# Entry of the feed-forward part of a decoder step: first token forms ahead of the first pair, the third tile on single banks, negated weight copies ahead of their casts

## The chip, the cores and the metric

The kernel runs on one core of one Trainium2 chip. The metric is the time of one execution in device microseconds (us), lower is better; three executions of the kernel before gave a median of 1043.3 us. A core has TensorE (PE, matrix products into PSUM banks), VectorE (DVE), ScalarE (ACT), GpSimd (POOL) and SyncE (SP); the last two issue transfers here, SP plain loads and POOL accumulating ones.

## The reference

One layer of a hybrid decoder trunk, for 512 prompt tokens and 8 sample tokens (520 columns in all), width 1024. After a mixing part of four branches and a cross attention it ends with

```
h3 = rms_norm(x, norm_ffn_g)
x = x + jnp.square(jax.nn.relu(h3 @ w_up)) @ w_down        # w_up 1024 x 4096, w_down 4096 x 1024
```

The change is at the beginning of this last line. Everything ahead of it, and the caches that the layer returns, is computed as before.

## The kernel before, in words

**Numbers in two parts.** Every matrix product is computed from a high and a low part of each factor (float32r): `wh` is the weight cast, `wl` the weight less `wh`, and likewise `hi` and `lo` for tokens. `mm3` (L260) does high by high, high by low, low by high, each for two halves of 260 columns: six products for one slice of 128 rows. A weight tile of 128 x 1024 has eight slices: 48 products.

**How weights come.** `weights` (L165) keeps LA = 3 tiles ahead in a fixed order: ..., `wxo` 0 to 3, `wup` 0 to 3, `wdn` 0, 2, 1, 3, then pairs. `split_weights` (L211) loads a tile `w` from SP and makes `wh` on ACT (L219). For most tiles DVE then subtracts (`low`, L178). For `wdn` ACT writes the negated weight, rounded to float32r, into `wl` behind the cast (L221, `scale=-1.0`), and a transfer issued by POOL adds the exact weight to it (L222, `accum_op=add`), so that the difference remains. Three buffers each for `w`, `wh` and `wl`: a tile's parts can be written when the tile three places earlier has been used.

**The entry of the feed-forward part** (L1527 to L1540). After the eight output tiles of `wxo`, whose residuals (L1190 to L1199) also give the token tiles `x2s`, `rstd` computes the norm's factor `Rf`. `pair` multiplies `wup` 0 and 1 slice by slice in turn into two tiles of the pool `pg` (two tiles of two PSUM banks each). `run` does `wup` 2 and then `wup` 3, each into a tile of `pg`. Each tile has a post-step, `post_up`: relu on ACT (L1423), times `Rf` on DVE (L1424), square on ACT (L1417), high and low part (L145, L146). A post-step is traced only when the next tile's products have been traced (`take`, `advance`). Then `down(0, c)` multiplies the four resulting token slices with `wdn` c; each weight tile has two halves n = 0 and 1, into a tile of `pg` and into two single banks of the pool `pm` (three banks in all).

**Token forms.** From the second group on, `up_pair` computes two `wup` tiles at once from sums and differences of token quarters. `forms` (L1392) prepares them in four steps, each with two multiplications (L1396), four additions (L1404 to L1407) and four splits into high and low parts. The steps are traced with `next(made)`: the first between the pair and the third tile, the second between the third and the fourth, the others behind.

**What sets the order.** A planner orders the instructions of each engine ahead of the run, by simulating them with costs of its own: of those that are ready it takes the one with the highest priority, which is the place in the trace. Inside `tc.high_priority(offset=60)` the place counts as 60 earlier; nested, the offsets add up. `advance` traces a post-step in such a block, and `pin` ties DVE instructions that were traced behind the first DVE instruction of a post-step to stay behind it, except those in `free` (the weight subtractions). On the chip each engine then runs its list strictly in order. In the planned list of the kernel before, `wdn` 0 has only its first two slices (24 products) ahead of the first slices of `wdn` 2; its third and fourth follow.

Of the kernel before, what the change touches and what calls it, by code (L numbers as in the profile page):

```python
# [12 lines left out]
AF = mybir.ActivationFunctionType  # L13
ALU = mybir.AluOpType
# [12 lines left out]
AHEAD = 60  # L27
# [70 lines left out]
def layer(ctx: ExitStack, tc: tile.TileContext, I: dict, O: dict):  # L98
    nc = tc.nc
    V, S, PE, SP, GP = nc.vector, nc.scalar, nc.tensor, nc.sync, nc.gpsimd  # L100
# [11 lines left out]
    def gtile():  # L112
        return pg.tile([P, 2, 512], F32, tag="g", name="g")

    def mtile():
        return pm.tile([P, 512], F32, tag="m", name="m")

    def dtile():
        return pd.tile([P, 512], F32, tag="d", name="d")
# [4 lines left out]
    def HL(dt=F32R, shape=None):  # L124
        return hp.tile(shape or [P, NT], dt, tag="hl", name="hl", bufs=HLB)
# [8 lines left out]
    def two(t):  # L134
        return t[:, 0:NT].rearrange("p (a b) -> p a b", a=2)

    def gv(ps):
        return ps[:, :, 0:H2]
# [38 lines left out]
    def low(wl, w, wh):  # L177
        free.add(V.tensor_tensor(out=wl, in0=w, in1=f(wh), op=ALU.subtract).ins.name)  # L178
# [32 lines left out]
    def split_weights(name, i):  # L211
        if name == "pair":
            return split_pair(i)
        src = I[name][i]
        w = wp.tile([P, KT, P], F32, tag="w", name="w", bufs=WB[0])
        SP.dma_start(out=w, in_=src.rearrange("p (k c) -> p k c", k=KT))
        wh = wp.tile([P, KT, P], F32R, tag="wh", name="wh", bufs=WB[1])
        wl = wp.tile([P, KT, P], F32R, tag="wl", name="wl", bufs=WB[2])
        S.copy(wh, w)  # L219
        if name == "wdn":  # L220
            S.activation(wl, w, AF.Copy, scale=-1.0)  # L221
            GP.dma_start(out=wl, in_=src.rearrange("p (k c) -> p k c", k=KT), accum_op=ALU.add)  # L222
        else:
            low(wl, w, wh)
        return wh, wl

# [32 lines left out]
    def mm3(outs, wh, wl, xh, xl, first, last):  # L259

        for n, (w, x) in enumerate(((wh, xh), (wh, xl), (wl, xh))):
            for o, sl in outs:
                m = PE.matmul(o, lhsT=w, rhs=x[sl], start=first and n == 0, stop=last and n == 2)  # L263
        return m
# [4 lines left out]
    def banks(ps):  # L269
        return [p[:, 0:H2] for p in ps] if isinstance(ps, list) else [ps[:, i, 0:H2] for i in range(2)]  # L270

    def gemm(ps, W, xs, first=True, last=True, k0=0, apart=False):

        wh, wl = W
        outs = [(p, sl) for p, sl in zip(banks(ps), (A0, A1))]
        for o in [outs[:1], outs[1:]] if apart else [outs]:
            for i, (xh, xl) in enumerate(xs):
                PE_last[0] = mm3(o, wh[:, k0 + i], wl[:, k0 + i], xh, xl, first and i == 0, last and i == len(xs) - 1)
# [59 lines left out]
    ps = dtile()  # L338
# [4 lines left out]
    halves = (slice(0, H2), slice(H2, NT))  # L343
# [33 lines left out]
    def Rtile():  # L377
        return tp.tile([P, NT], F32, tag="R", name="R", bufs=1)
# [40 lines left out]
    def advance():  # L419

        fresh[0] = False
        new = pending[-1]
        pin()
        n = len(nc.cur_bb.bb.instructions)
        with tc.high_priority(offset=AHEAD):
            alive = next(new, True) is None
            evac[0] = next((i for i in nc.cur_bb.bb.instructions[n:] if i.engine == mybir.EngineType.DVE), evac[0])
        pending[:] = onward(pending[:-1]) + [new] * alive
        flows[:] = onward(flows)
# [14 lines left out]
    def take(post):  # L444

        if fresh[0]:
            advance()
        pending.append(post)
        fresh[0] = True

    def run(name, i, src, post, steps=0, k0=0, W=None, apart=False):

        ps = [mtile(), mtile()] if apart else gtile()
        W = W or weights(name, i)
        gemm(ps, W, src, k0=k0, apart=apart)
        take(post(ps))
        step(steps)
        return W

    def pair(names, src, posts):  # L460

        ps = [gtile() for n in names]
        Ws = [weights(*n) for n in names]
        for k in range(KT):
            for p, (wh, wl) in zip(ps, Ws):
                gemm(p, (wh[:, k:], wl[:, k:]), src[k:k + 1], first=k == 0, last=k == KT - 1)
        for p, post in zip(ps, posts):
            take(post(p))
# [162 lines left out]
    def step(n=1):  # L631
        for _ in range(n):
            next(dec, None)
# [589 lines left out]
    pss = dtile()  # L1223
# [138 lines left out]
    x2, x2s = [None] * KT, [None] * KT  # L1362
# [15 lines left out]
    Rf = Rtile()  # L1378
    ups = [[None] * 4 for g in range(8)]
# [11 lines left out]
    def forms():  # L1391

        for k in range(4):
            n, m, t, u = T(), T(), T(), T()
            for o, i in ((n, k), (m, k + 4)):
                V.scalar_tensor_tensor(out=o, in0=x2[i], scalar=col("gffn", i), in1=Rf, op0=ALU.mult, op1=ALU.mult)  # L1396
            B11, B12, B21, B22 = n[:, A0[1]], n[:, A1[1]], m[:, A0[1]], m[:, A1[1]]
            if k % 2 == 0:
                b11 = form(2)
            sl = slice(k % 2 * H2, k % 2 * H2 + H2)  # L1400
            hilo(B11, b11[0][:, sl], b11[1][:, sl])
            X["B11", k] = b11[0][:, sl], b11[1][:, sl]
            N1, T2, T3, T4 = t[:, A0[1]], t[:, A1[1]], u[:, A0[1]], u[:, A1[1]]
            V.tensor_tensor(out=N1, in0=B11, in1=B12, op=ALU.subtract)  # L1404
            V.tensor_tensor(out=T2, in0=B22, in1=N1, op=ALU.add)
            V.tensor_tensor(out=T3, in0=B22, in1=B12, op=ALU.subtract)
            V.tensor_tensor(out=T4, in0=T2, in1=B21, op=ALU.subtract)  # L1407
            for src, names in ((t, ("N1", "T2")), (u, ("T3", "T4")), (m, ("B21", "B22"))):
                hi, lo = form(2)
                hilo(src, hi, lo)  # L1410
                for j, s in zip(names, (A0[1], A1[1])):
                    X[j, k] = hi[:, s], lo[:, s]
            yield

    def rest(r, hl):

        S.activation(r, r, AF.Square)  # L1417
        hilo(r, *hl)

    def post_up(i):  # L1420
        def post(ps):
            r = T()
            S.activation(two(r), gv(ps), AF.Relu)  # L1423
            V.tensor_tensor(out=r, in0=r, in1=Rf, op=ALU.mult)  # L1424
            ups[0][i] = HL(), HL()
            rest(r, ups[0][i])
            yield
        return post

# [54 lines left out]
    def post_down(g, c):  # L1484
        def post(ps):
            t = x2[c]
            if isinstance(ps, list):
                for p, sl in zip(banks(ps), halves):
                    V.tensor_tensor(out=t[:, sl], in0=p, in1=t[:, sl], op=ALU.add)
                    if g == 7 and c == KT - 1:  # L1490
                        SP.dma_start(out=O["yT"][c][:, sl], in_=t[:, sl])
            else:
                V.tensor_tensor(out=two(t), in0=gv(ps), in1=two(t), op=ALU.add)
            if g == 7 and c < KT - 1:
                SP.dma_start(out=O["yT"][c], in_=t)
            yield
        return post

    def down(g, cp):

        W = weights("wdn", 4 * g + cp)
        cs = (2 * cp, 2 * cp + 1)
        pss = [gtile(), [mtile(), mtile()]]

        def part(n, ks, first, last):
            for i, k in enumerate(ks):
                gemm(pss[n], (W[0][:, 4 * n:], W[1][:, 4 * n:]), ups[g][k:k + 1], first=first and i == 0,
                     last=last and i == len(ks) - 1, k0=k)

        if cp == CP[0]:  # L1510
            late = 2 if g else 3
            for n in range(2):
                part(n, [k for k in range(4) if k != late], True, False)
            for n in range(2):
                part(n, (late,), False, True)
                take(post_down(g, cs[n])(pss[n]))
        elif g == 7 and cp == CP[-1]:
            part(0, range(4), True, True)
            take(post_down(g, cs[0])(pss[0]))
            gemm(pss[1], (W[0][:, 4:], W[1][:, 4:]), ups[g], apart=True)  # L1520
            take(post_down(g, cs[1])(pss[1]))
        else:
            for n in range(2):
                part(n, range(4), True, True)
                take(post_down(g, cs[n])(pss[n]))
# [2 lines left out]
        rstd(ones, [acc], D, T(), Rf)  # L1528
    first_pair = split_pair(2)
    made = forms()  # L1530
    pair([("wup", 0), ("wup", 1)], x2s, [post_up(0), post_up(1)])
    next(made)
    run("wup", 2, x2s, post_up(2))
    next(made)
    run("wup", 3, x2s, post_up(3))
    go()
# [109 lines left out]
```

## Time and profile before

| | us |
|---|---|
| median of three runs | 1043.3 (1042.77 to 1044.19) |
| profiled execution, whole | 1040.07 |
| its span, first to last instruction | 1038.4 |
| PE busy in it | 1020.9 (98%) |
| DVE busy | 669.4 (64%) |
| ACT busy | 525.8 (51%) |
| POOL busy | 170.3 (16%) |

The page's times come from one profiled execution; the run's own time lies 1.67 us above the span. In the views by order of time each line begins with the start and the duration in us, and a bracket at its end says how long the engine had been idle and what released it. The feed-forward part takes the stretch from about 683 us to the end; its entry, with the four `wup` tiles, that from 683 to about 707.

### The profile page before, as it was taken

What the parts mean: (1) busy time and instruction counts of PE and PEld (TensorE: products, weight loads), DVE (VectorE), ACT (ScalarE), POOL (GpSimd) and SP (SyncE); (2) the same over time, 40 slices, a digit from 0 to 9 for tenths busy, and PEclk for the clock granted to TensorE, in tenths of its full rate; (3) what the DMA queues carried; (4) which work ended last, traced back from release to release, by engine and by line L of the source; (5) the groups of instructions that cost most, each with busy time, mean ns of one, the idle gap of its engine ahead of it and who ended that gap; (6) DMA issues with size and microseconds to landing.
All of it is one profiled execution on the core that took longest, in us unless ns stands there. A gap on an engine that the chain in (4) does not pass through costs nothing.

```text
span 1038.4 us, 21502 instructions
## 1 busy us (share of the span) xinstructions
PE 1020.9 (98%) x8266; PEld 941.1 (91%) x8266; DVE 669.4 (64%) x1231; ACT 525.8 (51%) x858; POOL 170.3 (16%) x299
## 2 busy tenths in 40 slices
PE   8999999999999999999999999999999999999998
PEld 7978787888988898889999986899999999999998
DVE  6766766776556665534676678689756566566643
ACT  7756567854222225412545577567636355363541
POOL 1333442231223332230100000000001000010000
PEclk9999999999999999999999999999999999999999
DMA  8877986574457776772523548146457564565544
GB/s 264 339 235 253 260 284 199 194 224 153 154 192 244 243 231 218 221 248 88 195 82 103 187 163 286 74 132 151 125 143 162 142 163 123 145 162 142 122 103 123
DMA packets 62089, 188.87 MB, mean 182 GB/s; under 512 B 10145, under 2 KB 12962, under 8 KB 61858
## 3 DMA queue, kind: packets, MB, share of 16 engines
q0 software_dynamic: 25408, 84.97, 30.7%
q1 hardware_dynamic: 36578, 102.52, 29.0%
q8 instruction: 65, 1.06, 0.4%
q14 instruction: 38, 0.31, 0.1%
HBM read 181.85 MB, written 5.61 MB: 181 GB/s over the span
## 4 chain that ended last, share of the span: by engine, by line
PE 89%; ACT 4%; DVE 4%; DMA 1%; issue 1%; SPq 0%; DVEq 0%; ACTq 0%
PE g L263 60%; PE m L263 15%; PE d L600 3%; PE d L548 2%; PE d L263 2%; PE m L286 2%; PE g L1171 1%; ACT wh L219 1%; DVE wl L178 1%; DMA wl<-in_wdn 1%; DMA hl<-in_xT 1%; PE m L653 1%; PE m L701 0%; PE m L687 0%; PE m L708 0%
## 5 line engine op out<-in xcount | busy, mean ns | idle before, releaser
L263 PE MATMUL g<-hl,wh 128*128 128x260 f32 x3664 | 606.6, 285 | 3.9 <-DVE sd L570 1.5
L263 PEld LDWEIGHTS g<-hl,wh 128*128 128x128 f32 x3664 | 510.3, 188 | 22.2 <-issue 7.0
L263 PE MATMUL g<-hl,wl 128*128 128x260 f32 x1832 | 384.6, 283 | 1.7 <-DMA wl<-in_wdn 1.7
L263 PEld LDWEIGHTS g<-hl,wl 128*128 128x128 f32 x1832 | 288.4, 188 | 2.2 <-DMA wl<-in_wdn 1.9
L219 ACT CAST wh<-w 128x1024 fp32r<-128x1024 f32 x126 | 132.0, 1048 | 283.6 <-PE g L263 115.8
L178 DVE TENSOR_TENSOR wl<-w,wh 128x1024 fp32r<-128x1024 f32 (+1 forms) x122 | 141.3, 1160 | 37.1 <-ACT wh L219 33.9
L263 PE MATMUL m<-hl,wh 128*128 128x260 f32 x792 | 134.8, 282 | 0.0
L263 PEld LDWEIGHTS m<-hl,wh 128*128 128x128 f32 x792 | 114.0, 188 | 0.0
L222 POOL DMA_DIRECT2D wl<-in_wdn x32 | 27.7, 866 | 491.2 <-DVE t L1396 196.0
L513 POOL DMA_DIRECT2D pg<-in_vc x128 | 69.0, 539 | 176.1 <-issue 79.4
L513 POOL DMA_DIRECT2D pg<-in_kc x128 | 69.3, 541 | 145.7 <-issue 100.1
L263 PE MATMUL m<-hl,wl 128*128 128x260 f32 x396 | 92.4, 282 | 0.0
L475 DVE TENSOR_TENSOR t<-g,R 128x520 f32<-128x520 f32 x48 | 33.4, 695 | 64.1 <-PE g L263 64.1
L263 PEld LDWEIGHTS m<-hl,wl 128*128 128x128 f32 x396 | 66.2, 188 | 0.0
L146 DVE TENSOR_TENSOR hl<-t,hl 128x520 fp32r<-128x520 f32 (+3 forms) x67 | 43.6, 654 | 20.6 <-ACT hl L145 20.2
L197 ACT CAST wh<-p 128x1024 fp32r<-128x1024 f32 x28 | 29.4, 1049 | 40.4 <-PE m L263 28.1
L145 ACT CAST hl<-t 128x520 fp32r<-128x520 f32 (+3 forms) x67 | 39.0, 589 | 18.3 <-DVE t L486 11.3
L197 ACT CAST wh<-w 128x1024 fp32r<-128x1024 f32 (+1 forms) x28 | 23.3, 835 | 39.8 <-PE m L263 30.1
L882 DVE SCALAR_TENSOR_TENSOR hl<-uc,cols,hl 128x512 f32<-128x512 f32 x60 | 41.2, 746 | 0.0
L178 DVE TENSOR_TENSOR wl<-p,wh 128x1024 fp32r<-128x1024 f32 x28 | 34.3, 1224 | 7.9 <-ACT wh L197 7.9
L191 DVE TENSOR_TENSOR p<-w 128x512 f32<-128x512 f32 x28 | 19.0, 688 | 26.6 <-DMA w<-in_wup 26.6
L221 ACT ACTIVATE wl<-w 128x1024 fp32r<-128x1024 f32 x32 | 33.7, 1054 | 0.0
(301 smaller groups left out, 1156.7 us busy)
## 6 DMA issues: line engine op xcount, KB each, us to landing
pg<-in_kc POOLq DMA_DIRECT2D x128, 256.0 KB, 4.5
pg<-in_vc POOLq DMA_DIRECT2D x128, 256.0 KB, 3.9
w<-in_win SPq DMA_DIRECT2D x56, 512.0 KB, 4.5
w<-in_wup SPq DMA_DIRECT2D x32, 512.0 KB, 3.5
w<-in_wdn SPq DMA_DIRECT2D x32, 512.0 KB, 3.6
wl<-in_wdn POOLq DMA_DIRECT2D x32, 512.0 KB, 7.8
w<-in_wo SPq DMA_DIRECT2D x8, 512.0 KB, 3.2
hl<-in_cmk SPq DMA_DIRECT2D x16, 256.0 KB, 5.2
```

Of the source, the lines that this page charges most:

```text
L145: S.copy(hi, src)
L146: V.tensor_tensor(out=lo, in0=src, in1=f(hi), op=ALU.subtract)
L178: free.add(V.tensor_tensor(out=wl, in0=w, in1=f(wh), op=ALU.subtract).ins.name)
L197: S.copy(h, src)
L219: S.copy(wh, w)
L221: S.activation(wl, w, AF.Copy, scale=-1.0)
L222: GP.dma_start(out=wl, in_=src.rearrange("p (k c) -> p k c", k=KT), accum_op=ALU.add)
L263: m = PE.matmul(o, lhsT=w, rhs=x[sl], start=first and n == 0, stop=last and n == 2)
L475: V.tensor_tensor(out=two(t), in0=gv(ps), in1=two(Rt), op=ALU.mult)
L513: last.append(GP.dma_start(out=dst, in_=src[bass.ds(pid, 1)].rearrange("o p f -> p o f")))
L600: PE.matmul(ps[32 * i:32 * i + 32, :], lhsT=Dt[:, n, :], rhs=vp[:, i, :], start=n == 0, stop=n == 15)
L882: V.scalar_tensor_tensor(out=y[:, 0:NP], in0=u[:, k:k + NP], scalar=cw[:, k:k + 1], in1=y[:, 0:NP], op0=ALU.mult, op1=ALU.add)
```

## The change

`wup` 1 and 2 get their low part like `wdn` does, from a negated copy and an accumulating transfer; and where that is done, copy and transfer are traced ahead of the cast. The first step of the forms is traced ahead of the pair. The third tile goes to two single banks of `pm` (the parameter `apart`, which also split the order of the products and was not used here, gives way to `single`). `post_up` reads either kind of tile, and its instructions stand in a further high-priority block inside that of `advance`. In the first down tile of a group, the slices of group 0 go in three rounds, (0, 1), (2), (3), each over both halves, where it was (0, 1, 2) and (3); later groups keep (0, 1, 3) and (2).

```
-        S.copy(wh, w)
-        if name == "wdn":
+        added = name == "wdn" or (name == "wup" and i in (1, 2))
+        if added:
             S.activation(wl, w, AF.Copy, scale=-1.0)
             GP.dma_start(out=wl, in_=src.rearrange("p (k c) -> p k c", k=KT), accum_op=ALU.add)
-        else:
+        S.copy(wh, w)
+        if not added:
             low(wl, w, wh)
...
-        ps = [mtile(), mtile()] if apart else gtile()
+        ps = [mtile(), mtile()] if single else gtile()
         W = W or weights(name, i)
-        gemm(ps, W, src, k0=k0, apart=apart)
+        gemm(ps, W, src, k0=k0)
...
             r = T()
-            S.activation(two(r), gv(ps), AF.Relu)
-            V.tensor_tensor(out=r, in0=r, in1=Rf, op=ALU.mult)
-            ups[0][i] = HL(), HL()
-            rest(r, ups[0][i])
+            with tc.high_priority(offset=AHEAD):
+                if isinstance(ps, list):
+                    for p, sl in zip(banks(ps), halves):
+                        S.activation(r[:, sl], p, AF.Relu)
+                else:
+                    S.activation(two(r), gv(ps), AF.Relu)
+                V.tensor_tensor(out=r, in0=r, in1=Rf, op=ALU.mult)
+                ups[0][i] = HL(), HL()
+                rest(r, ups[0][i])
             yield
...
-            late = 2 if g else 3
-            for n in range(2):
-                part(n, [k for k in range(4) if k != late], True, False)
-            for n in range(2):
-                part(n, (late,), False, True)
-                take(post_down(g, cs[n])(pss[n]))
+            parts = ((0, 1, 3), (2,)) if g else ((0, 1), (2,), (3,))
+            for ks in parts:
+                for n in range(2):
+                    part(n, ks, ks is parts[0], ks is parts[-1])
+                    if ks is parts[-1]:
+                        take(post_down(g, cs[n])(pss[n]))
...
     made = forms()
+    next(made)
     pair([("wup", 0), ("wup", 1)], x2s, [post_up(0), post_up(1)])
-    next(made)
-    run("wup", 2, x2s, post_up(2))
+    run("wup", 2, x2s, post_up(2), single=True)
     next(made)
     run("wup", 3, x2s, post_up(3))
```

## Rows read from the trace of the kernel before

**Rows 1.** The page's first part: busy us, share of the span, instructions.

```profile
PE 1020.9 (98%) x8266; PEld 941.1 (91%) x8266; DVE 669.4 (64%) x1231; ACT 525.8 (51%) x858; POOL 170.3 (16%) x299
```

**Rows 2.** Stretches: length, busy us of each engine, granted clock, queues' share, GB/s.

```profile
696.00:714.00 18.00, 16.28 (x134) 16.08 (x135) 17.75 (x35) 16.58 (x28) 2.63 (x3) 1.00 0.72 161
...
750.00:1038.00 288.00, 285.20 (x2376) 284.98 (x2374) 168.85 (x296) 133.20 (x174) 22.50 (x26) 1.00 0.57 138
```

**Rows 3.** Waits of PE, 640 to 1038: for whom, us, times, longest.

```profile
PE g L263 <- DMA wl<-in_wdn: 1.7, 1, 1.7
PE g L263 <- ACT t L1423: 0.7, 1, 0.7
```

**Rows 4.** PE in order of time: the pair's end and the third tile's start.

```profile
693.62 0.64 PE L263 MATMUL g<-hl,wh 128*128 128x260 f32 x4
...
694.35 0.65 PE L263 MATMUL g<-hl,wh 128*128 128x260 f32 x4
...
695.90 0.74 PE L263 MATMUL g<-hl,wh 128*128 128x260 f32 x4 [0.67 <-ACT t L1423]
```

**Rows 5.** PE in order of time: the first products of `wdn` 2.

```profile
710.38 0.64 PE L263 MATMUL g<-hl,wh 128*128 128x260 f32 x4
712.73 0.51 PE L263 MATMUL g<-hl,wl 128*128 128x260 f32 x2 [1.72 <-DMA wl<-in_wdn]
```

**Rows 6.** The chain that ended last, in time: start, us, what (issue to landing).

```profile
705.72 6.97 DMA wl<-in_wdn
```

**Rows 7.** ACT in order of time: `wdn` 2's cast and copy, third relu.

```profile
702.57 1.05 ACT L219 CAST wh<-w 128x1024 fp32r<-128x1024 f32 x1
...
704.36 1.06 ACT L221 ACTIVATE wl<-w 128x1024 fp32r<-128x1024 f32 x1
705.32 0.58 ACT L1423 ACTIVATE t<-g 128x520 f32<-128x520 f32 x1
```

**Rows 8.** DVE in order of time: norm's factor, a weight subtraction, first post-step.

```profile
692.02 0.70 DVE L299 SCALAR_TENSOR_TENSOR R<-t 128x520 f32<-128x520 f32 x1
695.38 1.23 DVE L178 TENSOR_TENSOR wl<-w,wh 128x1024 fp32r<-128x1024 f32 x1 [2.65 <-ACT wh L219]
696.52 0.69 DVE L1424 TENSOR_TENSOR t<-t,R 128x520 f32<-128x520 f32 x1
```

**Rows 9.** DVE in order of time: low parts of the third and fourth tokens.

```profile
709.05 0.69 DVE L146 TENSOR_TENSOR hl<-t,hl 128x520 fp32r<-128x520 f32 x1
...
711.00 0.69 DVE L146 TENSOR_TENSOR hl<-t,hl 128x520 fp32r<-128x520 f32 x1
```

**Rows 10.** ACT in order of time: the cast of `wup` 1 and what follows.

```profile
676.91 1.05 ACT L219 CAST wh<-w 128x1024 fp32r<-128x1024 f32 x1
...
678.82 0.63 ACT L1198 ACTIVATE t<-x 128x520 f32<-128x520 f32 x1
```

**Rows 11.** PE in order of time: the first six products of `wup` 1.

```profile
684.02 0.64 PE L263 MATMUL g<-hl,wh 128*128 128x260 f32 x4
684.50 0.52 PE L263 MATMUL g<-hl,wl 128*128 128x260 f32 x3
```

**Rows 12.** L222, issue to landing: all 32, that at 720.4, that at 1003.5.

```profile
DMA to landing us min/median/max: 5.4/7.8/8.6
...
DMA to landing us min/median/max: 7.9/7.9/7.9
...
DMA to landing us min/median/max: 5.4/5.4/5.4
```

**Rows 13.** SP in order of time: plain weight loads issued.

```profile
680.59 0.33 SPq L216 DMA_DIRECT2D w<-in_wdn  x1
...
705.44 0.33 SPq L184 DMA_DIRECT2D w<-in_wup  x1
...
720.05 0.33 SPq L216 DMA_DIRECT2D w<-in_wdn  x1
...
1000.66 0.33 SPq L216 DMA_DIRECT2D w<-in_wdn  x1
```

More of the change, by code (lines that the diff above doesn't have):

```diff
@@ L449, in take, with run @@
         fresh[0] = True
-    def run(name, i, src, post, steps=0, k0=0, W=None, apart=False):
-        ps = [mtile(), mtile()] if apart else gtile()
+    def run(name, i, src, post, steps=0, k0=0, W=None, single=False):
+        ps = [mtile(), mtile()] if single else gtile()
         W = W or weights(name, i)
-        gemm(ps, W, src, k0=k0, apart=apart)
+        gemm(ps, W, src, k0=k0)
         take(post(ps))
```

## The prediction

> **What bounds the kernel now.** I read the page's first part, then the stretches, the waits of TensorE behind 640 us, and only then the engines in order of time around the entry of the feed-forward part. The first part has TensorE (PE) busy nearly throughout, the other engines at most two thirds [rows 1]. From 750 us to the end its products stand back to back at the granted clock 1.00, its higher level of 2.4 GHz [rows 2]: what is won or lost ahead of that point reaches the end undiminished. So only PE's waits count. Two of them lie at the entry: 0.7 us for the first tile's relu and 1.7 us for the negated weights of a `wdn` tile [rows 3]. Those two are what the change can take away, and as matmul ends are modelled I size both by starts. Six products take 0.72 to 0.73 us (693.62 to 694.35), 0.12 each [rows 4].
>
> - Wait A: the pair's last group starts at 694.35, so the third `wup` tile was due at 695.07 and started at 695.90: **0.83 us**. Both double-bank tiles of `pg` were held by the pair until ScalarE (ACT) had read the first [rows 3, 4].
> - Wait B: the four high products start at 710.38, so the first low one was due at 710.86 and started at 712.73: **1.87 us** [rows 5]. That is the second down weight (`wdn` 2; the order is 0, 2, 1, 3), whose accumulating transfer was issued at 705.72 and landed 6.97 us later, at 712.69 [rows 6].
>
> **The change part by part.**
>
> *Third tile on single banks.* It takes two tiles of `pm` and no longer needs the pair's relu: wait A goes, −0.83. The relu becomes two instructions for one of 0.58 us [rows 7], at most 0.6 us more on ACT, beside 5.8 us of the fourth tile's products. What is late next is that tile's weights, and they are given the same room as before relative to the pair's end. The fourth tile needs the double bank of the first, free with the relu some 5 us before.
>
> *First forms ahead of the pair, the post-step at doubled priority.* No instruction is added. VectorE (DVE) had the norm's factor at 692.72 (692.02 + 0.70) and then stood idle 2.65 us, because the forms were traced behind the first tile's post-step and pinned behind its multiply at 696.52 [rows 8]. Now they can fill that hole. By itself this is worth nothing on PE: the third tile's tokens were complete at 709.74 and the fourth's at 711.69 [rows 9], while PE could have begun the third slice of `wdn` 0 at 710.38 at the earliest and, twelve products on, the last at 711.82. The tokens were in time; it was the issue order that had `wdn` 2 ahead of them. What the part changes is that order. I cost it at nothing; were it to delay the first post-step by a whole form (2.65 us of cover gone), the tokens of the first slices are still due only 11.5 us behind the pair.
>
> *Slices (0,1), (2), (3) and the negated copy ahead of the cast.* The two go together against wait B. ACT did the cast of `wdn` 2 at 702.57, two casts of forms behind it, and the negated copy only at 704.36 [rows 7]: the copy first starts the transfer at least 1.05 us sooner. And with tokens ready for the planner, all 48 products of `wdn` 0 (5.76 us) stand ahead of `wdn` 2, not 24. Third tile from 695.07 to 700.83, fourth to 706.59, `wdn` 0 to 712.35, low product of `wdn` 2 due at 712.83 (all plus the stall below). The transfer landed 11.03 us behind the end of the third tile (712.69 less 701.66); the same distance is 711.86, or 710.8 with the copy first. It is in time by 1 to 2 us: −1.87. If only the third slice comes ahead, it is due at 711.39, still between those two.
>
> *`wup` 1 and 2 by negated copy and accumulating transfer.* This removes two DVE subtractions of 1.23 us [rows 8], which DVE could spare (PE waits for none of them), and adds two ACT copies of 1.06 us [rows 7], two issues on GpSimd (POOL) and 1 MB through the queues. ACT has idle time there, so the copies cost nothing by themselves. The landing does. `wup` 2 finds its buffers one weight later, 5.8 us on at 682.7, and is due 12 us behind that: harmless. `wup` 1 is the second tile of the pair itself. Its buffers come free with the third `wxo` weight; ACT started its cast at 676.91 [rows 10]. Now the copy starts there: ready at 677.97, issued 0.30 us later as at wait B (copy done at 705.42, issue at 705.72) [rows 6, 7], 678.27. Its first low product ran at 684.50 [rows 11]. Issue to landing over all 32 such transfers is 5.4 to 8.6 us [rows 12]: landed between 683.7 and 686.9, a stall of **0 to 2.4 us**. Which end? The change also lets SyncE (SP) send the first `wdn` load at about 679.0 (677.97 and 1.05 for the cast) rather than 680.59, since the load's buffer now waits for a cast and not for a subtraction [rows 13]; so one plain load runs beside it. With one such load beside, issued within 0.4 us, the transfers took 7.0 and 7.9; the one at 1003.5, with the last plain weight load issued at 1000.66, took 5.4 [rows 6, 12, 13]. I take 7.5: landed 685.77, product at 685.81 with the 0.04 us that wait B shows (712.69 to 712.73), stall **1.3 us**.
>
> Would the planner see that and put the first tile's products ahead? In the order of before it set the low product of `wdn` 2 76 products (9.1 us) behind the end of the third tile, with its copy ending 3.76 us behind that end; so my estimate is that it counts at most 5.3 us from copy to landing, where the chip took 7.3. For `wup` 1 that is 683.3, ahead of 684.50: it keeps the order, and PE waits. Everything behind shifts with it, the sums above too, so the margins stay. The granted clock was 1.00 through wait B's stretch too [rows 2]; so a shorter stall is costed at its length alone.
>
> Here the Trainium skill speaks for the change. Its page "DMA: Bandwidth & Descriptors", section "Anatomy of one DMA — SWDGE (gpsimd) path", fits a transfer issued by GpSimd as about 2.0 us plus its bytes over 436 GB/s; for 512 KB that is an estimate of 3.2 us, landed at 681.5, no stall and a sum of −2.7 us. The trace disagrees by these rows (none of 32 accumulating ones under 5.4 us), so the result it gives stands below as a rival only.
>
> **Sum:** −0.83 − 1.87 + 1.3 = **−1.4 us**. Against the profiled execution (1040.07 us, its span 1038.4 and 1.67 around it) that is 1038.7. The median of the runs is 3.2 us above that execution; the same −1.4 on it gives **1041.9**.
>
> **The rivals.**
>
> 1. *No stall.* The transfer takes the 5.4 us of the undisturbed one, or the planner, seeing it late, lets the first tile's remaining 42 products (5.0 us) run ahead. Then −2.7: **1040.6**. For: the shortest time seen is enough (683.7 against 684.50), and the queue was free of other loads but one. Against: that one load.
> 2. *The order of `wdn` 2 stays.* The change doesn't do what it says for wait B, as the tokens are still late in the planner's reckoning, where ACT has two copies more to do. Then at most the whole 1.87 remains: −0.83 + 1.3 = +0.5, **1043.8**. Against: 2.65 us of DVE freed.
> 3. *Slower.* The negated copy of `wup` 1 goes behind the fifth residual's two ACT operations, which end at 679.45 [rows 10], because it now has to find both its buffer and the planner's turn. Then it is ready at 680.51, issued 680.81, and with 8.6 us lands at 689.41: a stall of 4.9 us, −2.7 + 4.9 = +2.2, **1045.5**. It decides from a landing behind 687.2 on, where the stall exceeds both waits. Against: ACT took the cast at once at 676.91, with equal priority.
>
> **How the numbers follow.** Forecast 0.45, rival 1 0.25, rival 2 0.15, rival 3 0.12, other orderings 0.03. The forecast's own range, from a stall of 0.6 to 2.4, is 1041.2 to 1043.0. A measurement of this kernel tells 0.2% from no change, 2.1 us: 1041.2 and 1045.4. Below the first lie four fifths of rival 1 (0.20) and 0.08 of the forecast: faster 0.28. Above the second lie three quarters of rival 3 and the odd ones: slower 0.12. The rest, 0.60, is within. The range leaves out a tenth at each end: from 1040.2, rival 1 with 0.4 us for the stray of a median (the three runs lie 1.4 apart), to 1044.9, between rivals 2 and 3.
>
> **What would show it.** In the waits of PE behind 640 us: no wait for the relu of L1423 (now another line); no wait for `wl<-in_wdn`; a new one for `wl<-in_wup` of about 1.3 us, at 684.5. In POOL's order of time: two issues at about 678.3 and 684. On DVE: the forms of the first token slice starting at about 692.7 plus the stall. In ACT's order: each negated copy ahead of its cast, from `wdn` 0 on. The prediction is wrong if `wl<-in_wup` never stops PE, if it stops it for over 2.4 us, or if a wait stands at the down products that was not there before, such as the single banks being asked for by `wdn` 0 while the third tile's halves are unread.

## The result, and the profile after

The changed kernel is **slower**: 1051.88 us (median of 4 runs, 1051.66 to 1055.17) against 1043.03 us of the kernel before on the same chip (4 runs, 1041.18 to 1044.19), a ratio of 1.0098 with a 95% interval of 1.0082 to 1.0114. The prediction, 1041.9 in a range of 1040.2 to 1044.9, was wrong in sign and by 10 us. The profiled execution took 1051.72 us, its span 1050.0: 11.6 us more than the one of before. The traces lie further apart than the medians (8.9 us) because the profiled execution of before, at a mean granted clock of 1.00, is 3.0 us under that kernel's median, while that of the changed kernel (0.995) is at its own.

The page's first part (beside [rows 1]) hardly shows it. PE is busier by 6.6 us with the same 8266 instructions, and DVE by 3 us less:

```profile
PE 1027.5 (98%) x8266; PEld 945.4 (90%) x8266; DVE 666.3 (63%) x1229; ACT 526.8 (50%) x861; POOL 171.9 (16%) x301
```

The waits of PE behind 640 us tell where to look (waiting line and what ended the wait; us, times, longest). Both rows of [rows 3] are gone. In their place stand one wait for the accumulating transfer of a `wup` tile, and five for a residual addition of VectorE:

```profile
PE m L264 <- DVE hl L1495: 5.2, 5, 1.8
PE g L264 <- DMA wl<-in_wup: 3.6, 1, 3.6
```

**The stall at the pair.** PE in order of time, beside [rows 4, 11]; behind the stall six products take 1.2 to 1.3 us where they took 0.72:

```profile
684.36 0.64 PE L264 MATMUL g<-hl,wh 128*128 128x260 f32 x4
688.58 0.63 PE L264 MATMUL g<-hl,wl 128*128 128x260 f32 x3 [3.58 <-DMA wl<-in_wup]
689.04 0.95 PE L264 MATMUL g<-hl,wh 128*128 128x260 f32 x4
...
690.23 1.07 PE L264 MATMUL g<-hl,wh 128*128 128x260 f32 x4
...
700.82 0.64 PE L264 MATMUL m<-hl,wh 128*128 128x260 f32 x4
```

The stretches around it, with the columns of [rows 2]: granted clock and the queues' share are the two numbers ahead of the last.

```profile
684.00:689.00 5.00, 1.42 (x12) 1.21 (x11) 4.37 (x7) 2.55 (x4) 0.86 (x1) 1.00 0.99 229
689.00:692.00 3.00, 3.00 (x17) 3.00 (x16) 0.00 (x0) 0.00 (x0) 0.00 (x0) 0.53 0.99 317
692.00:695.00 3.00, 3.00 (x21) 2.81 (x21) 0.00 (x0) 2.02 (x4) 0.00 (x0) 0.90 0.28 108
695.00:698.00 3.00, 3.00 (x27) 3.00 (x27) 1.96 (x3) 0.90 (x2) 0.00 (x0) 1.00 0.00 0
```

What is to be seen: the low product was due at 684.84, four high ones behind 684.36, and came at 688.58, **3.74 us** late. Behind it the granted clock is 0.53, its lower level of 1.2 GHz, until into the next stretch. The third tile starts at 700.82 with no wait, where 695.07 was its due time in the kernel before. Of these 5.75 us, 0.34 lie ahead of the pair (684.36 against 684.02 [rows 11]), 3.74 are the stall, and the remaining **1.7** are the clock.

Why the transfer was late stands in three orders of time and the chain. ACT and SP (beside [rows 10, 13]), then POOL:

```profile
677.24 1.05 ACT L223 CAST wh<-w 128x1024 fp32r<-128x1024 f32 x1
678.19 1.06 ACT L221 ACTIVATE wl<-w 128x1024 fp32r<-128x1024 f32 x1
```

```profile
679.28 0.33 SPq L216 DMA_DIRECT2D w<-in_wdn  x1
680.36 0.33 SPq L184 DMA_DIRECT2D w<-in_wup  x1
```

```profile
679.57 0.90 POOL L222 DMA_DIRECT2D wl<-in_wup  x1 [178.09 <-ACT wl L221]
```

The chain of waits (start, issue to landing; beside [rows 6]), and all transfers of L222 in the feed-forward part (beside [rows 12]):

```profile
679.57 8.97 DMA wl<-in_wup
```

```profile
DMA to landing us min/median/max: 5.1/7.6/9.0
```

On this tile the cast still stands ahead of the copy: the planner kept that order although the trace order is the other. The transfer took 8.97 us, more than any of the 32 of before (8.6), with two plain loads beside it, one of them the first pair's.

**The five later waits.** One place of the five, in order of time. ACT, POOL, the chain (the second load of a pair, issue to landing), DVE and PE of the changed kernel:

```profile
755.27 1.04 ACT L221 ACTIVATE wl<-w 128x1024 fp32r<-128x1024 f32 x1
756.22 0.61 ACT L145 CAST hl<-t 128x520 fp32r<-128x520 f32 x1
756.73 1.05 ACT L223 CAST wh<-w 128x1024 fp32r<-128x1024 f32 x1
```

```profile
756.67 0.87 POOL L222 DMA_DIRECT2D wl<-in_wdn  x1 [17.08 <-ACT wl L221]
```

```profile
757.81 6.82 DMA w<-in_wup
```

```profile
764.65 0.69 DVE L191 TENSOR_TENSOR p<-w 128x512 f32<-128x512 f32 x1 [4.88 <-DMA w<-in_wup]
765.26 0.69 DVE L1499 TENSOR_TENSOR hl<-g,hl 128x520 f32<-128x520 f32 x1
765.87 0.75 DVE L1495 TENSOR_TENSOR hl<-m,hl 128x260 f32<-128x260 f32 x2
```

```profile
766.34 0.62 PE L264 MATMUL m<-hl,wh 128*128 128x260 f32 x3 [1.18 <-DVE hl L1495]
```

And the same place in the kernel before: ACT, SP, POOL, DVE.

```profile
751.68 1.03 ACT L219 CAST wh<-w 128x1024 fp32r<-128x1024 f32 x1
...
753.14 1.05 ACT L221 ACTIVATE wl<-w 128x1024 fp32r<-128x1024 f32 x1
```

```profile
752.18 2.37 SPq L184 DMA_DIRECT2D w<-in_wup  x2
```

```profile
754.72 0.87 POOL L222 DMA_DIRECT2D wl<-in_wdn  x1 [17.53 <-DVE hl L146]
```

```profile
757.71 0.69 DVE L191 TENSOR_TENSOR p<-w 128x512 f32<-128x512 f32 x1 [1.48 <-DMA w<-in_wup]
```

How to read it. The second load of an odd pair goes into one of the three buffers `w` of the down tiles. Before, the last reader of that buffer was the negated copy (ended 754.19), which released load and transfer alike: SP's second load went out at 754.22 (its row ends at 754.55 and one issue takes 0.33), the transfer 0.5 us behind it. After, the copy releases the transfer early (756.67), and the cast, now last, releases the load at 757.81. So the 512 KB transfer is ahead of the load in the queues, and DVE can start on the load 6.84 us behind its issue instead of 3.49. DVE, in order, stands at the sum L191 that needs the load; the residual additions that read out the single banks of `pm` stand behind it; PE waits for a bank. DVE waited at that sum before too, 26.6 us over 11 times and after 40.1, but until then it cost PE nothing.

The same reading at all six such places (worked out from SP's, POOL's, DVE's and PE's rows; us; the landing is counted from the load's issue to the start of DVE's sum, 0.02 to 0.03 behind the landing itself):

```
             load issued   transfer issued   load's landing   PE's wait
before       754.22        754.72 (+0.50)    3.49             -
             797.48        797.80 (+0.32)    3.83             -
             840.64        840.97 (+0.33)    5.18             -
             883.91        884.23 (+0.32)    4.40             -
             927.21        927.54 (+0.33)    5.05             -
             970.47        970.81 (+0.34)    3.61             -
after        757.81        756.67 (-1.14)    6.84             1.18
             802.49        801.36 (-1.13)    6.12             0.51
             846.40        845.27 (-1.13)    7.42             1.75
             893.17        892.17 (-1.00)    6.70             1.05
             937.75        936.61 (-1.14)    6.29             0.65
             981.87        980.74 (-1.13)    5.48             -
```

PE's wait is the landing less 5.65, within 0.05 us, at each; no landing of before reached that. By 742.56 us the 5.75 of the entry are down to 3.56: waits A and B (2.70) are not there, and 0.5 is not placed. From pair to pair the distance between the two kernels (first product of each group's bank `d`) shows what the waits cost: +3.56 at 742.56, then +5.05, +5.77, +9.30, +10.57, +11.41, +11.57, and +11.61 at the last product (1046.52 against 1034.91). That is **8.0 us** behind the entry: 5.2 of waits, 0.2 to 0.3 more at each by starts, and in the step of 3.53 again about 1.6 of clock. The stretches behind the wait of 1.75:

```profile
855.00:858.00 3.00, 2.49 (x15) 2.50 (x16) 3.00 (x7) 0.38 (x1) 0.00 (x0) 0.74 0.69 143
858.00:862.00 4.00, 4.00 (x28) 4.00 (x28) 3.36 (x5) 1.72 (x2) 0.00 (x0) 0.77 0.27 52
```

### The profile page after: what moved, and what is told of

Same layout as the page of the kernel before. It is cut to its first block, busy times and chain, and to the rows that moved or that the text cites. A ratio compares the mean times of both kernels' runs of the same rounds, so it can differ in the third digit from the quotient of the medians.

```text
span 1050.0 us, 21496 instructions
## 1 busy us (share of the span) xinstructions
PE 1027.5 (98%) x8266; PEld 945.4 (90%) x8266; DVE 666.3 (63%) x1229; ACT 526.8 (50%) x861; POOL 171.9 (16%) x301
## 3 DMA queue, kind: packets, MB, share of 16 engines
q8 instruction: 65, 1.06, 0.4%
## 4 chain that ended last, share of the span: by engine, by line
PE 74%; ACT 8%; DVE 6%; DMA 6%; issue 5%; SPq 0%; DVEq 0%; ACTq 0%; POOLq 0%
PE g L264 50%; PE m L264 12%; DMA w<-in_wup 3%; PE d L601 3%; PE d L549 2%; PE m L287 1%; DMA w<-in_win 1%; DVE wl L178 1%; ACT wh L223 1%; PE d L264 1%; PE g L1172 1%; ACT wl L221 1%; DMA wl<-in_wup 1%; DVE t L1453 1%; DVE hl L146 1%
## 5 line engine op out<-in xcount | busy, mean ns | idle before, releaser
L178 DVE TENSOR_TENSOR wl<-w,wh 128x1024 fp32r<-128x1024 f32 (+1 forms) x120 | 138.8, 1157 | 34.6 <-ACT wh L223 31.7
L264 PE MATMUL m<-hl,wh 128*128 128x260 f32 x824 | 142.4, 285 | 5.2 <-DVE hl L1495 5.2
L264 PEld LDWEIGHTS m<-hl,wh 128*128 128x128 f32 x824 | 119.9, 190 | 6.2 <-DVE hl L1495 6.2
L264 PE MATMUL m<-hl,wl 128*128 128x260 f32 x412 | 96.6, 285 | 0.0
L222 POOL DMA_DIRECT2D wl<-in_wdn x32 | 27.6, 864 | 319.3 <-ACT wl L221 207.6
L264 PEld LDWEIGHTS m<-hl,wl 128*128 128x128 f32 x412 | 69.6, 190 | 0.0
L146 DVE TENSOR_TENSOR hl<-t,hl 128x520 fp32r<-128x520 f32 (+3 forms) x67 | 43.5, 652 | 20.6 <-ACT hl L145 20.2
L191 DVE TENSOR_TENSOR p<-w 128x512 f32<-128x512 f32 x28 | 19.0, 686 | 40.1 <-DMA w<-in_wup 40.1
L883 DVE SCALAR_TENSOR_TENSOR hl<-uc,cols,hl 128x512 f32<-128x512 f32 x60 | 41.2, 744 | 0.0
```

The lines of the kernel that those rows point to most:

```text
L146: V.tensor_tensor(out=lo, in0=src, in1=f(hi), op=ALU.subtract)
L883: V.scalar_tensor_tensor(out=y[:, 0:NP], in0=u[:, k:k + NP], scalar=cw[:, k:k + 1], in1=y[:, 0:NP], op0=ALU.mult, op1=ALU.add)
```

## The experiments

All times are medians; "before" stands for runs of the kernel before taken with each batch (1042.31 us for experiments 1 to 4, 1042.61 for 5 to 8, 1042.26 for 9 to 12), and each ratio is to it. The first four take the two suspects apart: the `wup` transfers and the copy ahead of the cast. In what was written ahead of the seventh to the ninth, "buffer theory" means that the load is released too late, "queue theory" that the transfer ahead of it holds it up.

**1. Cast ahead of the copy again, `wup` 1 and 2 still by transfer.**

```
+        S.copy(wh, w)
         if added:
             S.activation(wl, w, AF.Copy, scale=-1.0)
             GP.dma_start(...)
-        S.copy(wh, w)
```

> The changed kernel with the cast of each weight ahead of its negated copy again; wup 1 and 2 still get their low part by transfer. Two theories of the five waits of PE for the residual addition L1495, one in each of five later groups (5.1 us in the profile, and a stretch at 855 us at a lower granted clock that costs some 1.7 more). Theory LOAD: copy-first makes the cast the last reader of w and sends the accumulating transfer ahead of SP's next load, so the pair's weight lands late, VectorE stands in its list at L191 and the residual behind it frees its bank late. Then they go here, and what stays is the stall for wup 1 (3.7 us, about 1 us more as the copy starts a cast later, and 1.7 for the clock) less the two waits won: 3 to 4.5 us slower than before. Rival ORDER: the waits come from the other parts (places in the trace that shifted); then they stay, 9 to 11 us slower than before.

1046.93 us, ratio 1.0043 (1.0028 to 1.0058). The five waits are gone, the stall stays, and a wait for the transfer of `wdn` 0 stands at the down tiles (PE at 713.11, 48 products behind the fourth tile's start):

```profile
PE g L268 <- DMA wl<-in_wup: 3.9, 1, 3.9
PE g L268 <- DMA wl<-in_wdn: 1.6, 1, 1.6
```

**2. `wup` 1 and 2 subtracted on DVE again, copy first for all `wdn`.**

```
-        added = name == "wdn" or (name == "wup" and i in (1, 2))
+        added = name == "wdn"
```

> The changed kernel with wup 1 and 2 subtracted on VectorE as before; the copy stays ahead of the cast for wdn. The stall of 3.6 us for wup 1 and the stretch at the lower granted clock behind it (about 0.5 from 689 to 692 us, some 1.7 us) go: 5.4 us less than the changed kernel by either theory of the later waits, 3 to 5 us slower than before. If the clock fell for another reason than the stall, 3.7 less.

1047.48 us, ratio 1.0056 (1.0039 to 1.0074). Nothing stops PE at the entry, the five waits are there:

```profile
PE m L268 <- DVE hl L1499: 4.8, 5, 1.8
```

The traced execution took 1042.45 us at a mean granted clock of 1.00; the other five took 1046.6 to 1050.9 at 0.995 to 0.998. The trace shows the waits, but not all of what the median loses.

**3. Both taken back** (the edits of 1 and 2).

> The changed kernel with both taken back: wup 1 and 2 on VectorE, cast ahead of copy. What is left are the forms ahead of the pair, the doubled priority, the single banks and the three rounds of slices. Theory LOAD: both waits at the entry stay won and nothing is lost: 1 to 2.7 us faster than before (1.0 if the wait for wdn 2 returns in part, as its copy starts a cast later). Rival ORDER: the later waits stay: 3 to 5 us slower than before.

1042.44 us, ratio 1.0001 (0.9990 to 1.0011). So against before: both +8.9, the first alone +4.6, the second alone +5.2, none +0.1. The two causes nearly add up (9.8 for 8.9; only nearly, as 1 and 3 each have a wait at the down tiles that 2 has not), and without them nothing is lost. But what waits A and B cost is not won either, where 1 to 2.7 us were expected. With the cast first, ACT casts `wdn` 0 at 696.60 and copies it only at 700.00, behind token work; PE has come to it sooner, and stands there. ACT, then PE:

```profile
696.60 1.04 ACT L222 CAST wh<-w 128x1024 fp32r<-128x1024 f32 x1
...
700.00 1.06 ACT L224 ACTIVATE wl<-w 128x1024 fp32r<-128x1024 f32 x1
```

```profile
709.55 0.51 PE L268 MATMUL g<-hl,wl 128*128 128x260 f32 x2 [3.04 <-DMA wl<-in_wdn]
```

**4. The kernel before with the copy first for `wdn`, nothing else.**

```
-        S.copy(wh, w)
         if name == "wdn":
             S.activation(wl, w, AF.Copy, scale=-1.0)
             GP.dma_start(...)
+            S.copy(wh, w)
         else:
+            S.copy(wh, w)
             low(wl, w, wh)
```

> The kernel before with one edit: for wdn the negated copy and its transfer ahead of the cast. Theory LOAD: the waits for L1495 (its line in this kernel is 1489 plus the shift) appear in the later groups, 4 to 7 us slower, less up to 1 us of the wait for wdn 2. Rival ORDER: no such wait, 0 to 1 us faster than before.

1047.34 us, ratio 1.0050 (1.0031 to 1.0068): the one order does it, in either kernel. Wait B is gone and wait A (0.7) stays, so this order is enough to cure wait B; the five waits sum to 5.5 us.

```profile
PE m L268 <- DVE hl L1494: 5.5, 5, 1.7
```

Among the transfers around the later places the accumulating one alone has moved. Counted from the first product of each group's bank `d`, the pair's loads of the last five places go out within 0.06 us of where they did before (the first at 19.7 to 19.8, the second at 21.8), here, in experiment 2 and in the changed kernel. The transfer goes out at 20.6 to 20.8 instead of 22.1.

**5. Copy first only where it is wanted:** the changed kernel without `wup` transfers, and copy first for the four down tiles of the first group. Where `ahead_of_cast` is false, the cast is traced first.

```
+        added = name == "wdn"
+        ahead_of_cast = added and i < 4
```

> The changed kernel with wup 1 and 2 on VectorE and with the copy ahead of the cast for the first four wdn tiles alone; all later tiles have the cast first. If the price of copy-first lies in the later groups alone (theory LOAD), both waits at the entry stay won and nothing is lost: 2 to 2.7 us faster than before. Rival: once the wait for the relu is gone, the transfer of wdn 0 or 2 is late by as much, as in the run with both taken back (3.0 us): 0 to 1 us faster.

1038.84 us, ratio 0.9965 (0.9953 to 0.9978): **faster than both**. No wait of PE is left in the feed-forward part. From the third tile's due time to the last product its trace takes 337.54 us (697.27 to 1034.81), that of before 339.84 (695.07 to 1034.91): 2.3 of the 2.7 us of waits A and B. The medians differ by 3.8; the other 1.5 the traces don't place. (Spans of single executions aren't compared, because the third tile's due time lies anywhere from 693.6 to 697.3 in those that have no stall ahead of it. It goes with the granted clock ahead of the entry: 693.6 to 695.1 us in the traces without a stretch at the lower clock there (before, 2, 3, 7, 12), 695.3 to 695.8 with one (6, 8, 9, 11), 696.3 and 697.3 with two (4, 5; here 0.57 from 268 to 272 us and from 643 to 647, both 1.00 in before).)

**6. The fifth, and `wup` 2 by transfer.**

```
+        added = name == "wdn" or (name == "wup" and i == 2)
```

> The run before this one in the list, with wup 2 by negated copy and transfer again (wup 1 stays on VectorE). The prediction called wup 2 harmless: the same time within 0.5 us. Rival: the transfer and the additional copy on ScalarE put off others at the entry: 1 to 4 us slower than that run.

1040.50 us, ratio 0.9987 (0.9972 to 1.0002), 1.7 above the fifth. The two intervals overlap slightly, but the trace has a wait of that size. PE waits:

```profile
PE m L268 <- DMA wl<-in_wup: 1.8, 1, 1.8
```

ACT does the copy at 687.03, 4.0 us behind the cast, with two more casts and two token operations between; the transfer, issued at 688.41, took 9.33 us.

**7. The kernel before, copy first for all `wdn`, and two load buffers of their own for the odd pairs.**

```
-        w = [(wp if i % 2 else fp).tile(..., tag="w", bufs=WB[0] if i % 2 else 2) for _ in range(2)]
+        w = [fp.tile(..., tag="wq" if i % 2 else "w", bufs=2) for _ in range(2)]
```

> The kernel before with the copy first for every wdn tile, and two load buffers of their own for the pairs that shared the three of wdn. If the later waits come from the pair's weight landing late (theory LOAD), SP can send it without waiting for wdn's last reader, and the waits for the residual go: 5 us less than the same edit without the buffers, 0 to 1 us faster than before. Rival: the copy first disturbs in another way (ScalarE's order, the banks): 4 to 5 us slower stays.

1039.44 us, ratio 0.9972 (0.9959 to 0.9984): the five waits are gone, wait A alone is left. Compared with the fourth the buffers are worth 8.2 us, each against its own before. That is more than the 5.5 of the waits, and the 3.2 us below before are more than the 0 to 1 expected; what such buffers give with the cast first was not run.

**8. The kernel before, copy first, the cast held right behind it** on ACT.

```
+            neg = S.activation(wl, w, AF.Copy, scale=-1.0)
+            GP.dma_start(...)
+            with tc.high_priority(offset=AHEAD), tc.issue_after(neg.ins):
+                S.copy(wh, w)
```

> The kernel before with the copy first for every wdn tile, and the cast held directly behind it by priority. It tells two reasons for the late load apart. BUFFER: the cast, with its lower place, slips behind a token cast and is the last reader of w; then here w comes free as in the kernel before, 2.1 us behind the copy's start, and the waits go: 0 to 1 us faster than before. QUEUE: the accumulating transfer now enters the queues a microsecond ahead of the plain load and takes their time; then the waits stay: 4 to 5 us slower.

1042.51 us, ratio 0.9997 (0.9982 to 1.0012), between the two theories: one wait of the five is left, and 0.6 us of wait B.

```profile
PE m L266 <- DVE hl L1492: 1.5, 1, 1.5
```

The loads still go out 1.0 to 1.15 us behind the transfer and still land later than in the kernel before (3.5 to 5.2): 7.04, 5.59, 5.65, 5.98, 5.45, 5.46 us. Only the first is far beyond the 5.65 at which PE began to wait above, and only there PE waits. Why these landings are up to 1.8 us shorter than those of the changed kernel at nearly the same issue times isn't settled, but one other issue moved: the pair's first load, which at the four middle places goes out 1.35 us ahead of the transfer here and 0.9 to 1.0 us ahead there. In the four kernels with the copy first for every `wdn` and the old buffers (2, 4, 8, the changed one) the second load took 6.1 to 7.4 us where the first went out 0.9 to 1.1 us ahead of the transfer, and 5.4 to 6.0 where it was 1.35 us ahead or there was none, at the last place. No run moves it alone.

**9. The second with two load buffers of their own for the odd pairs** (the edit of 7).

> The changed kernel with wup 1 and 2 subtracted on DVE again, the negated copy ahead of the cast for all wdn tiles, and two load buffers of their own for the second weights of the pairs. Buffer theory (the cast is the last reader of the load buffer, the pair's load waits for it): with buffers of its own the load no longer waits for that cast, so the five waits of PE for the residual (4.8 us, and the loss of clock) go: 1038.9, the time of the kernel in which only the first four down tiles have the copy first, or up to 1 us under it. Rival (queue theory: the accumulating transfer ahead of the load holds it up, whoever frees the buffer): the waits stay, 1043 to 1047.

1039.29 us, ratio 0.9971 (0.9958 to 0.9984). The waits are gone, and what DVE waits at L191 falls from 41.2 us in the second to

```profile
  DMA w<-in_wup: 12.1, 5
```

That was the outcome the buffer theory named. Yet it doesn't decide: with buffers of their own the loads go out at other times too, and no `wup` load follows such a transfer closely any more (the nearest is 0.2 us ahead of it, at the first place 1.06). What decides is the table of six places. Shift the issues of before by the distance the two kernels have there (3.56, 5.05, 5.77, 9.30, 10.57, 11.41), and the loads of before stand at 757.78, 802.53, 846.41, 893.21, 937.78, 981.88: the changed kernel sent them at 757.81, 802.49, 846.40, 893.17, 937.75, 981.87. The buffer comes free at the same moment, since the cast now ends where the copy ended. Only the transfer moved, by 1.4 to 1.6 us, to the front (754.72 + 3.56 = 758.28 against 756.67). So the load is late by its flight and not by its release: the buffer theory falls, and the **queue theory** is what the table bears out; more buffers help by parting the two. It is not the whole of the landing's length, as experiment 8 shows.

**10. The fifth, and `wup` 1 by transfer.**

```
+        added = name == "wdn" or (name == "wup" and i == 1)
```

> The kernel with the copy first for the first four down tiles alone, and wup 1 (not wup 2) by negated copy and accumulating transfer. Theory that the whole entry stall is the transfer of wup 1 and costs its length (3.7 us) and the half clock behind it (1.7 us): 1038.8 + 5.4 = 1044.2. Rival (it is the two transfers together that made the landing late; alone it takes the 5.4 to 7 us of an undisturbed one): a stall of 0 to 1.3 us, 1038.8 to 1040.1.

1046.33 us, ratio 1.0039 (1.0025 to 1.0053), 7.5 above the fifth, more than expected. The traced execution took 1048.49 us, 2.2 above the median. The chain, PE and two stretches:

```profile
681.77 9.96 DMA wl<-in_wup
```

```profile
691.78 1.02 PE L268 MATMUL g<-hl,wl 128*128 128x260 f32 x3 [4.58 <-DMA wl<-in_wup]
```

```profile
692.00:695.00 3.00, 3.00 (x15) 3.00 (x16) 0.00 (x0) 0.00 (x0) 0.00 (x0) 0.50 0.87 296
695.00:698.00 3.00, 3.00 (x12) 2.62 (x12) 0.00 (x0) 0.87 (x2) 0.00 (x0) 0.52 0.08 30
```

The transfer is not late because there are two of them: alone it took 9.96 us, with a plain load issued 0.3 us ahead of it and one 0.8 us behind as in the changed kernel, and the lower clock lasted longer. From the last high products ahead of the stall (686.56) to the third tile's start (705.26) it is 18.70 us, where before took 11.05 (684.02 [rows 11] to 695.07): 4.74 of the difference are the stall by starts, the other 2.9 the clock.

**11. The fifth, third tile in a double bank again.**

```
-    run("wup", 2, x2s, post_up(2), single=True)
+    run("wup", 2, x2s, post_up(2))
```

> The kernel with the copy first for the first four down tiles alone, and the third tile in a double bank again. Theory (the single banks are worth the wait for the first relu, 0.83 us): that wait is back, 1038.8 + 0.8 = 1039.6. Rival (the wait costs nothing here, as something later in the entry waits anyway): 1038.8.

1038.74 us, ratio 0.9968 (0.9958 to 0.9978): the single banks are worth nothing that can be measured here. PE in order of time:

```profile
695.31 0.40 PE L268 MATMUL d<-x,wh 128*128 128x260 f32 x2
695.54 0.28 PE L268 MATMUL d<-x,wl 128*128 128x260 f32 x1
696.15 0.75 PE L268 MATMUL g<-hl,wh 128*128 128x260 f32 x4 [0.32 <-ACT t L1433]
```

The wait for the relu is 0.32 us, not 0.83. The planner has put products into bank `d` in the hole, which in the kernel before came at 719.58; the forms, now early, make them ready.

**12. The fifth, first forms behind the pair again.**

```
-    next(made)
     pair(...)
+    next(made)
```

> The kernel with the copy first for the first four down tiles alone, and the first step of the forms behind the pair again. The prediction costed this part at nothing by itself but gave it the order at the down tiles: if it decides that order, the weights of wdn 2 are waited for again, 0.5 to 1.9 us, 1039.3 to 1040.7. Rival (the copy ahead of the cast and the slices in three rounds do it without the forms): 1038.8.

1039.70 us, ratio 0.9975 (0.9963 to 0.9988). The interval overlaps that of the fifth, so the time doesn't tell. The trace shows two waits that the fifth doesn't have, 1.5 us together:

```profile
709.91 0.51 PE L268 MATMUL g<-hl,wl 128*128 128x260 f32 x2 [0.27 <-DMA wl<-in_wdn]
...
719.65 0.75 PE L268 MATMUL g<-hl,wh 128*128 128x260 f32 x4 [1.23 <-DVE hl L1503]
```

The first is the wait for `wdn` 2 that was expected, 0.27 us of the 0.5 to 1.9: PE comes to it at 709.00, 24 products behind the fourth tile's end, as in the kernel before, where in the fifth the third slice of `wdn` 0 comes first. So the forms' place does set that order, but with the copy first little hangs on it.

## Why the prediction was wrong

**The two waits at the entry: right.** A and B went, and with the two harmful parts out (experiment 5) 2.3 of the 2.7 us show in the trace. What was credited to each part was less right. For wait B the order of copy and cast is enough by itself (experiment 4; 0.6 us stay in 8). The order of `wdn` 2, which the forms' place does set, adds 0.27 (experiment 12). Wait A had a second cure, work for PE in the hole (experiment 11).

**The failed step: the negated copy ahead of the cast.** The prediction looked at it at one tile, as a transfer that starts "at least 1.05 us sooner", and took that as gain. The edit holds for all 32 `wdn` tiles. At the six odd pairs it turns the order of two releases round: the copy lets the transfer go, the cast the load, and DVE, and through it PE, needs the load first. Cost 8.0 us in the trace, +5.0 in the medians by itself, with wait B's cure in it (experiment 4), and 8.9 between experiments 5 and 2, each against its own before. The material stood in the trace of before: the wait of DVE at L191 of up to 3.23 us, and the transfer 0.3 us behind the load. "So only PE's waits count" was the sentence that kept me from reading it: a wait of DVE that costs nothing says how near the next one is, here 0.5 us at the landing of 5.18. I had listed "a wait at the down products" as what would prove me wrong, for a cause (single banks unread by the third tile) that was not the one.

**The stall of `wup` 1: right in place, 1.3 us sized, 3.74 measured.** Two terms were off. The issue came at 679.57 where the sum had 678.27: 0.33 lie upstream, and the other 0.97 is the cast, which ACT did ahead of the copy after all. And the landing took 8.97 for 7.5, with two loads beside it where I had counted one. 1.3 + 0.97 + 1.47 gives the 3.74. Rival 3 had nearly this landing (689.41 for 688.54), by another way; its point of decision, 687.2, was passed.

**The clock, put at nothing: wrong.** "A shorter stall is costed at its length alone" went by wait B, 1.72 us long, which had left the clock at 1.00 [rows 2]. The stall was not shorter: behind 3.58 us the clock stood at 0.53, and 1.7 us more went. Nor did a length near B's settle it, as the wait of 1.75 at 855 us shows (0.74 to 0.77, about 1.6 us).

**`wup` 2 "harmless": wrong** where PE isn't late already: +1.7 (experiment 6), at a wait of 1.76. The sum let ACT copy as soon as the buffers were free, at 682.7; the copy started at 687.03, and the transfer then took 9.33 us. In the changed kernel the stall of `wup` 1 hides it.

On the queues, the Trainium skill's page "DMA: Bandwidth & Descriptors", section "Issuing engines are not separate DMA queues", says that transfers of all issuing engines end up on the same 16 DMA engines and interleave. The trace agrees: at the six places a load issued by SP took 3.5 to 5.2 us ahead of POOL's transfer and 5.5 to 7.4 behind it. Had I weighed that rule against the copy's new place, it would have spoken against the change. The same page's fit for such a transfer, which the prediction set against the trace, gave 3.2 us; no accumulating transfer of these runs took under 5.1.

## What to carry to other kernels

When an instruction moves ahead of another that reads the same buffer, list what each of them releases: here the one let a transfer go and the other a load, and swapping them swapped the two in the queues, at six later places and not only at the tile that was looked at. Waits of an engine that is off the path are the measure of the slack: read how far the longest of them is from reaching the bound engine before adding traffic ahead of it. Make such a change only at the tiles that need it (experiment 5), or part the two by buffers (7, 9).

## What the runs showed of the hardware

- The accumulating transfer of `wup` 1, 512 KB with a plain load issued 0.3 us ahead of it and one 0.8 us behind, took 8.97 (the changed kernel), 9.24 (experiment 1) and 9.96 us (experiment 10) from issue to landing. Over the feed-forward part of the changed kernel such transfers took 5.1 to 9.0 us, plain loads of the same size 3.1 to 8.35.
- The clock behind a wait of PE isn't read off the wait's length alone. Behind waits of 3.0 to 4.6 us it fell to its lower level each time (granted 0.50 in experiments 1, 3 and 10 and 0.53 in the changed kernel, over 3 us), and 1.7 (changed kernel) and 2.9 us (experiment 10) more were lost. Behind waits of 1.72 (before, entry) and 1.76 (experiments 2 and 6) it stayed at 1.00; behind 1.75 at 855 us (the changed kernel) it fell. What told these apart the runs don't show.
